# Moving the up projection's results to feature partitions through DRAM, and weaving the up and down projections job by job

## Chip, cores and metric

The kernel runs on one core of a Trainium2 chip. The metric is the device time of one execution in microseconds (us), lower is better. The engines are named as the profile names them: PE is TensorE's matmul side and PEld its weight load, DVE is VectorE, ACT is ScalarE, POOL is GpSimd, and SP (SPq) is SyncE, which here issues every DMA.

## What is computed

One layer of an encoder for 256 tokens of width 2048. Attention and RWKV mixing come first, then a projection back to the residual stream `x`; the change touches only the last part, the MLP:

```
h2 = rms_norm(x, norm_mlp[l])                                     # (256, 2048)
u  = square(relu(einsum('btd,df->btf', h2, mlp_up[l])))           # (256, 8192)
x  = x + einsum('btf,fd->btd', u, mlp_down[l])                    # (256, 2048)
```

All inputs are float32. Products are made with float32r operands: each factor is split into a rounded part (`hi`) and a rest (`lo`), and one product is three matmuls, hi by hi, hi by lo and lo by hi.

## The kernel before

The program first records all operations (class `Recorder`), then `plan` (L195) sorts them into one order with a cost model of its own: for each engine it takes the operation that can start first, ties by rank. Each engine, and SP for the DMAs, then works through its list strictly in that order.

**Jobs.** Every weight matrix is cut into jobs of 256 rows by 512 columns (512 KB). `load` (L502) issues a job's DMA into one of four `raw` buffers. `split` (L517) makes from `raw` the rounded part `hi` on ACT and the rest `lo` on DVE, each in one of three buffers, and then calls `load` for a later job, which needs the `raw` buffer just read. Splitting runs two jobs ahead of PE (`LOOK`).

**Plain jobs and jobs in seven products.** A plain job is two row blocks by two token halves by three matmuls: 12 matmuls of 512 columns. For up groups 3 to 15 (`QUICK`), the jobs whose number stands in `FAST` are done by a scheme of Strassen's kind over a 2 x 2 grid of blocks: seven block products in place of eight, each again three matmuls, so 21 matmuls of 256 columns (`seven`, L545). For that, `split` also builds four sums of weight blocks `T` with three DVE subtractions, and splits them into `Th` (ACT) and `Tl` (DVE). The matching sums of activation blocks `S` are built once, in `normal_h` (L1449). Job 0 of each group stays plain.

**Up groups.** `up_group(i)` (L1480) is eight jobs and gives 512 columns of `u`, 256 tokens by 512 features, in PSUM banks: two for groups 0 to 2, four from group 3 on, which `join` (L1483) combines to `C` in SBUF. The next projection needs features on partitions, so the result has to be transposed. `f` (L1500) applies the relu and at the same time moves 32 x 32 blocks to other partitions: 32 instructions on 32 partitions of 128 elements each, 26 of them on ACT (`EV`) and 6 on DVE, into `z`. Later `fin` (L1519) transposes `z` within 32 x 32 blocks on DVE to `uf`, squares it and splits it to a unit of `u`.

**Down groups.** A down group is four plain jobs on two units of `u` for 512 columns of the output, in two PSUM banks, added to `x2` by DVE. The tag of the banks, `acc` or `side` with four banks each, changes from group to group, so that one group's banks are read while the next group's are written.

**Order.** The loop at the end (L1545) runs group after group: one up group (8 jobs), two down groups (4 jobs each), and again; six down groups come last. `rank = -SPL` puts the splitting ahead of other work that could start at the same time.

The SBUF pool `f` has 18 slots of 4 KB per partition, which `x2`, `S`, `T`, `Th`, `Tl`, `C`, `q`, `z` and `uf` share.

## Time and profile before

| what | value |
|---|---|
| median of 3 runs | 1191.83 us (1191.58 to 1193.58) |
| the profiled execution, its own time | 1192.01 us |
| its span | 1190.2 us |
| PE busy | 1179.4 us (99%) |
| DVE busy | 974.1 us (82%) |
| ACT busy | 844.8 us (71%) |
| DMA queue q1, share of 16 engines' span | 60.0% |
| granted TensorE clock | full in all of 40 slices |

Read it so: the span is what the profiler saw from the first to the last instruction, and the execution's own time is 1.8 us longer. Busy time of PE is modelled and says that it had work, not that each matmul ran at its peak. Idle time of an engine off the critical path costs nothing. Instruction durations of DVE and ACT overlap with the next instruction's start by about 0.08 us, so a row's mean is a little more than what one instruction takes of the engine.

### The profile page before, as it was taken

What the parts mean: (1) busy time and instruction counts of PE and PEld (TensorE: products, weight loads), DVE (VectorE), ACT (ScalarE), POOL (GpSimd) and SP (SyncE); (2) the same over time, 40 slices, a digit from 0 to 9 for tenths busy, and PEclk for the clock granted to TensorE, in tenths of its full rate; (3) what the DMA queues carried; (4) which work ended last, traced back from release to release, by engine and by line L of the source; (5) the groups of instructions that cost most, each with busy time, mean ns of one, the idle gap of its engine ahead of it and who ended that gap; (6) DMA issues with size and microseconds to landing.
All of it is one profiled execution on the core that took longest, in us unless ns stands there. A gap on an engine that the chain in (4) does not pass through costs nothing.

```text
span 1190.2 us, 18141 instructions
## 1 busy us (share of the span) xinstructions
PE 1179.4 (99%) x6649; PEld 979.9 (82%) x6649; DVE 974.1 (82%) x1579; ACT 844.8 (71%) x1421; POOL 7.3 (1%) x31
## 2 busy tenths in 40 slices
PE   9999999999999999999999999999999999999998
PEld 6887887888778778788888888888888888888886
DVE  7789594896975976798988988988988998898864
ACT  7784566855687768999686777687677677677652
POOL 2000000000000000000000000000000000000000
PEclk9999999999999999999999999999999999999999
DMA  8655656256455445656666666666666666666663
GB/s 279 205 159 164 172 162 184 85 165 175 128 169 172 141 142 184 180 169 194 188 198 199 184 203 198 194 190 197 212 176 196 198 192 182 208 180 197 207 205 132
DMA packets 126297, 216.20 MB, mean 182 GB/s; under 512 B 21824, under 2 KB 24384, under 8 KB 126208
## 3 DMA queue, kind: packets, MB, share of 16 engines
q1 hardware_dynamic: 126208, 215.05, 60.0%
q8 instruction: 52, 0.85, 0.3%
q14 instruction: 37, 0.30, 0.1%
HBM read 211.09 MB, written 3.93 MB: 181 GB/s over the span
## 4 chain that ended last, share of the span: by engine, by line
PE 77%; DVE 10%; ACT 7%; DMA 3%; issue 3%; SPq 0%; DVEq 0%; ACTq 0%
PE acc L334 47%; PE side L334 23%; DVE lo L334 4%; PE sm L334 3%; PE tr L334 3%; ACT z L334 2%; ACT hi L334 2%; DVE Tl L334 2%; DVE T L334 2%; PE sm L179 2%; DMA raw<-up 1%; DMA raw<-w_in 1%; DVE x L334 1%; DVE uf L334 0%; DVE u L334 0%
## 5 line engine op out<-in xcount | busy, mean ns | idle before, releaser
L334 DVE TENSOR_TENSOR lo<-raw,hi 128x1024 fp32r<-128x1024 f32 (+3 forms) x460 | 462.7, 1015 | 151.3 <-ACT hi L334 148.7
L334 ACT CAST hi<-raw 128x1024 fp32r<-128x1024 f32 (+2 forms) x395 | 405.0, 1033 | 164.2 <-PE acc L334 106.8
L334 PE MATMUL acc<-hi,xT 128*128 128x512 f32 (+1 forms) x832 | 267.6, 396 | 0.6 <-ACT hi L334 0.6
L334 PEld LDWEIGHTS acc<-hi,xT 128*128 128x128 f32 x832 | 154.6, 190 | 33.8 <-ACT hi L334 1.7
L334 PE MATMUL acc<-lo,xT 128*128 128x512 f32 (+1 forms) x416 | 164.0, 394 | 0.7 <-DVE lo L334 0.6
L334 PE MATMUL acc<-hi,u 128*128 128x512 f32 x512 | 163.2, 395 | 0.0
L334 PE MATMUL side<-hi,u 128*128 128x512 f32 x512 | 163.1, 395 | 0.0
L334 ACT ACTIVATE z<-C 32x128 f32<-32x128 f32 x338 | 104.2, 308 | 39.4 <-DVE C L334 35.0
L334 ACT CAST Th<-T 128x1024 fp32r<-128x1024 f32 x65 | 68.2, 1050 | 71.0 <-DVE T L334 70.3
L334 PEld LDWEIGHTS acc<-hi,u 128*128 128x128 f32 x512 | 96.4, 188 | 22.4 <-DVE u L334 0.3
L334 PEld LDWEIGHTS side<-hi,u 128*128 128x128 f32 x512 | 96.5, 188 | 22.2
L334 PE MATMUL side<-lo,u 128*128 128x512 f32 x256 | 101.0, 395 | 0.0
L334 PE MATMUL acc<-lo,u 128*128 128x512 f32 x256 | 101.0, 394 | 0.0
L334 PEld LDWEIGHTS acc<-lo,xT 128*128 128x128 f32 x416 | 78.9, 190 | 18.2 <-DVE lo L334 2.2
L334 PE MATMUL side<-hi,hN 128*128 128x512 f32 (+1 forms) x328 | 91.7, 353 | 0.0
L334 PE MATMUL acc<-hi,hN 128*128 128x512 f32 (+1 forms) x308 | 83.4, 343 | 0.0
L334 DVE TENSOR_TENSOR Tl<-T,Th 128x1024 fp32r<-128x1024 f32 x65 | 79.1, 1216 | 0.0
L334 PEld LDWEIGHTS side<-hi,hN 128*128 128x128 f32 x328 | 59.7, 188 | 9.5
L334 PEld LDWEIGHTS acc<-hi,hN 128*128 128x128 f32 x308 | 55.5, 188 | 7.8
L334 PE MATMUL side<-lo,hN 128*128 128x512 f32 (+1 forms) x164 | 57.9, 353 | 0.0
L334 PEld LDWEIGHTS acc<-lo,u 128*128 128x128 f32 x256 | 48.2, 188 | 11.0
L334 PEld LDWEIGHTS side<-lo,u 128*128 128x128 f32 x256 | 48.2, 188 | 11.0
(310 smaller groups left out, 1874.0 us busy)
## 6 DMA issues: line engine op xcount, KB each, us to landing
raw<-up SPq DMA_DIRECT2D x128, 512.0 KB, 3.8
raw<-down SPq DMA_DIRECT2D x128, 512.0 KB, 4.4
raw<-w_in SPq DMA_DIRECT2D x93, 512.0 KB, 3.8
raw<-w_out SPq DMA_DIRECT2D x32, 512.0 KB, 3.9
raw<-w_in SPq DMA_DIRECT2D x8, 288.0 KB, 3.1
x<-x SPq DMA_DIRECT2D x4, 512.0 KB, 7.3
out<-x SPq DMA_DIRECT2D x8, 256.0 KB, 3.4
raw<-w_in SPq DMA_DIRECT2D x6, 256.0 KB, 5.8
```

Of the source, the lines that this page charges most:

```text
L179: p.fn(*p.args, **p.kw)
L334: op.fn(*op.args, **op.kw)
```

## The change

- `FAST` grows from five of the eight jobs to seven; only job 0 stays plain. Two more tiles `S` are built, and the first two lie in tiles of an earlier stage (`HOME`), not in pool `f`.
- `f` now applies the relu with one ACT instruction per token half (128 partitions by 512) into `zr`, writes `zr` to a DRAM tile `Zd` with two DMAs, and reads it back with four DMAs of 32 partitions each, in runs of 128 elements, into `z`. The 32 block instructions are gone, and `EV` with them. `fin` transposes and splits as before, but reads and writes in runs of 32 elements where the layout now differs.
- `gemm` becomes a generator `steps` that pauses after each job. From up group 3 on, the eight jobs of an up group and the eight of two down groups are woven by the string `WEAVE` (u for an up job, d for a down job): d d u d u d u u d u d u d u d u. Up groups have the `acc` banks and down groups the `side` banks, always.
- The last two additions of `join` become one instruction of 512 elements, and all of `join` gets the rank of the splitting.

```
--- before.py
+++ after.py
@@ -32,8 +32,7 @@
 NF = 18
 NRAW = 4
 LOOK = 2
-EV = 13
-FAST = (1, 2, 4, 5, 7)
+FAST = (1, 2, 3, 4, 5, 6, 7)
 QUICK = 3
 
 SPL = 120
@@ -476,7 +475,6 @@
                 advance(t)
 
     w_in, w_out, w_up, w_dn = A["w_in"], A["w_out"], A["up"], A["down"]
-    turn = [0]
 
     jobs = []
     cols = [(c + 512 * h, 512) for h in range(2) for c in (4096, 3072, 5120)] + [(c + 512 * h, 512) for h in range(2) for c in (0, 1024, 2048)]
@@ -491,12 +489,18 @@
     def fast(job):
         return job[0] is w_up and job[2] >= 512 * QUICK and job[1] // 256 in FAST
 
-    jobs += up_jobs(0) + up_jobs(1)
-    for e in range(8):
-        for j in range(4):
-            if e < 7 and not j % 2:
-                jobs += up_jobs(2 * e + 2 + j // 2)
-            jobs += [(w_dn, e * 1024 + 256 * k, 512 * j, 512) for k in range(4)]
+    def down_jobs(d):
+        return [(w_dn, d // 4 * 1024 + 256 * k, d % 4 * 512, 512) for k in range(4)]
+
+
+    WEAVE = "ddududuududududu"
+    for i in range(3):
+        jobs += up_jobs(i)
+    for i in range(3, 16):
+        ups, downs = up_jobs(i), down_jobs(2 * i - 6) + down_jobs(2 * i - 5)
+        jobs += [(ups if c == "u" else downs).pop(0) for c in WEAVE]
+    for d in range(26, 32):
+        jobs += down_jobs(d)
     raws, parts = deque(), deque()
 
     def load(between=None):
@@ -552,7 +556,7 @@
             return [u[:, i, k + kk, t * P:(t + 1) * P] for i in range(2)]
 
         def s(i):
-            return [S[:, j, i] for j in range(2)]
+            return [S[j][:, i] for j in range(2)]
 
         def b(kk, n):
             return [x[:, kk, n * 256:n * 256 + 256] for x in (hi, lo)]
@@ -568,10 +572,13 @@
             nc.tensor.matmul(o, x[0], y[1], start=False, stop=False, skip_group_check=True)
             nc.tensor.matmul(o, x[1], y[0], start=False, stop=end, skip_group_check=True)
 
-    def gemm(units, w, c0, ncols, evac, side=False, hooks={}, off=0):
-        turn[0] += w is w_up or w is w_dn
+    def gemm(*args, **kw):
+        for _ in steps(*args, **kw):
+            pass
+
+    def steps(units, w, c0, ncols, evac, side=False, hooks={}, off=0, tag="acc"):
         quick = [j for j in range(8) if fast((w, 256 * j, c0))]
-        acc = [bank("side" if turn[0] % 2 else "acc") for _ in range(4 if quick else 2)]
+        acc = [bank(tag) for _ in range(4 if quick else 2)]
         nu = 4 if w is not w_out and w is not w_dn else 2
         nh = 2 * nu
         for j in range(nh):
@@ -586,8 +593,7 @@
             if j in quick:
                 seven(acc, units[j // 2], 2 * j % 4, sums_[FAST.index(j)], (hi, lo, *T_), j == quick[0], j == quick[-1])
                 done(2)
-                continue
-            for kk in range(2):
+            for kk in range(0 if j in quick else 2):
                 k = 2 * j + kk
                 u = units[off + j // 2]
                 for t in range(2):
@@ -598,7 +604,10 @@
                     nc.tensor.matmul(o, xh, hi[:, kk, :ncols], start=(k == 0), stop=False, **more)
                     nc.tensor.matmul(o, xh, lo[:, kk, :ncols], start=False, stop=False, **more)
                     nc.tensor.matmul(o, xl, hi[:, kk, :ncols], start=False, stop=(k == 2 * nh - 1), **more)
+            if j < nh - 1:
+                yield
         evac(acc)
+        yield
 
     def rsqrt_small(out, ss, scale, bias):
 
@@ -1432,6 +1441,7 @@
         squares(x2[j], parts2, j)
 
     rows2 = []
+    HOME = {0: ("DW", "DA"), 1: ("X", "Sp")}
 
     def rstd_rows():
 
@@ -1457,14 +1467,19 @@
         for p in range(2):
             if 2 * j + p in FAST:
 
-                S, sr = ftile([P, 2, 4, P], "S", F32R), ftile([P, 4, P], "sr")
+                sr = ftile([P, 4, P], "sr")
+                if len(sums_) in HOME:
+                    S = [sm.tile([P, 512], F32R, tag=g, bufs=1, name=nm("S")).rearrange("p (s t) -> p s t", s=4) for g in HOME[len(sums_)]]
+                else:
+                    S = ftile([P, 2, 4, P], "S", F32R)
+                    S = [S[:, 0], S[:, 1]]
                 a1, a2 = a[:, 2 * p], a[:, 2 * p + 1]
                 nc.vector.tensor_add(sr[:, 0], a1[:, P:], a2[:, P:])
                 nc.vector.tensor_sub(sr[:, 1], sr[:, 0], a1[:, :P])
                 nc.vector.tensor_sub(sr[:, 2], a1[:, :P], a1[:, P:])
                 nc.vector.tensor_sub(sr[:, 3], a2[:, :P], sr[:, 1])
-                nc.scalar.copy(S[:, 0], sr)
-                nc.vector.tensor_sub(S[:, 1], sr, S[:, 0])
+                nc.scalar.copy(S[0], sr)
+                nc.vector.tensor_sub(S[1], sr, S[0])
                 sums_.append(S)
                 done()
         done()
@@ -1477,7 +1492,7 @@
     us = []
     pend = []
 
-    def up_group(i, hooks):
+    def up_group(i, hooks, tag="acc"):
 
 
         def join(acc):
@@ -1485,6 +1500,7 @@
             C, q = ftile([P, 2, 512], "C"), ftile([P, 3, 256], "q")
             lt, rt = slice(0, 256), slice(256, 512)
             b0, b1, b2, b3 = acc
+            nc.rank = -SPL
             nc.scalar.copy(q[:, 0], b2[:, lt])
             nc.vector.tensor_add(q[:, 2], q[:, 0], b2[:, rt])
             nc.vector.tensor_add(q[:, 1], q[:, 2], b3[:, lt])
@@ -1492,41 +1508,38 @@
             nc.vector.tensor_add(C[:, 0], qf[:, :512], b0)
             nc.vector.tensor_add(C[:, 1, lt], q[:, 2], b1[:, lt])
             nc.vector.tensor_add(C[:, 1, rt], q[:, 1], b1[:, rt])
-            nc.vector.tensor_add(C[:, 1, lt], C[:, 1, lt], b3[:, rt])
-            nc.vector.tensor_add(C[:, 1, rt], C[:, 1, rt], b3[:, rt])
+            c1 = C[:, 1].rearrange("p (n c) -> p n c", n=2)
+            nc.vector.tensor_add(c1, c1, b3[:, rt].unsqueeze(1).broadcast_to([P, 2, 256]))
+            nc.rank = 0
             done()
             return C
 
         def f(acc):
-            z = ftile([P, 4, 2, 4, 32], "z")
+            zr, z, Zd = ftile([P, 2, 512], "zr"), ftile([P, 8, P], "z"), dr.tile([T, 512], F32, name=nm("Zd"))
             C = join(acc) if i >= QUICK else None
             for t in range(2):
-                for tb in range(4):
-                    rows = slice(32 * tb, 32 * tb + 32)
-                    src = (C[:, t] if C is not None else acc[t]).rearrange("p (f c i) -> p f c i", c=4, i=32)
-                    for cb in range(4):
-                        o, s = z[32 * cb:32 * cb + 32, :, t, tb, :], src[rows, :, cb, :]
-                        r = rstd2[rows, t:t + 1]
-                        if 4 * tb + cb < EV:
-                            nc.scalar.activation(o, s, AF.Relu, **({} if i > 1 else dict(scale=r)))
-                        elif i > 1:
-                            nc.vector.tensor_scalar(o, s, 0.0, None, op0=ALU.max)
-                        else:
-                            nc.vector.tensor_scalar(o, s, r, 0.0, op0=ALU.mult, op1=ALU.max)
-            if C is not None:
-                done()
+                a = (C[:, t] if C is not None else acc[t]).rearrange("p (f c i) -> p c f i", c=4, i=32)
+                o = zr[:, t].rearrange("p (c f i) -> p c f i", c=4, i=32)
+                nc.scalar.activation(o, a, AF.Relu, **({} if i > 1 else dict(scale=rstd2[:, t:t + 1])))
+                nc.sync.dma_start(Zd[t * P:(t + 1) * P, :], zr[:, t])
+            Zv = Zd.rearrange("(g l) (c n) -> c l g n", l=32, c=4)
+            for c in range(4):
+                nc.sync.dma_start(z[32 * c:32 * c + 32], Zv[c])
+            done(1 if C is None else 2)
 
             def fin():
                 u = unit("u")
                 us.append(u)
-                uf = ftile([P, 4, T], "uf")
-                nc.vector.transpose(uf.rearrange("p f t -> p (f t)"), z.rearrange("p f t b i -> p (f t b i)"))
+                uf = ftile([P, 8, P], "uf")
+                nc.vector.transpose(uf.rearrange("p g n -> p (g n)"), z.rearrange("p g n -> p (g n)"))
                 nc.scalar.activation(uf, uf, AF.Square)
-                nc.scalar.copy(u[:, 0], uf)
-                nc.vector.tensor_sub(u[:, 1], uf, u[:, 0])
+                v = uf.rearrange("p g (f i) -> p f g i", i=32)
+                u0, u1 = (u[:, a].rearrange("p f (g i) -> p f g i", i=32) for a in range(2))
+                nc.scalar.copy(u0, v)
+                nc.vector.tensor_sub(u1, v, u0)
                 done(2)
             pend.append(fin)
-        gemm(hN if i > 1 else hT, w_up, 512 * i, 512, f, hooks=hooks)
+        return steps(hN if i > 1 else hT, w_up, 512 * i, 512, f, hooks=hooks, tag=tag)
 
     def store_evac(j):
         def f(acc):
@@ -1539,14 +1552,26 @@
         while pend:
             pend.pop(0)()
 
-    up_group(0, {2: lambda: make_h(3), 4: rstd_rows})
-    up_group(1, {2 * j: lambda j=j: normal_h(j) for j in range(4)})
+    def down_group(d):
+        e, j = d // 4, d % 4
+        return steps(us, w_dn, 512 * j, 512, store_evac(j) if e == 7 else add_evac(x2[j]), hooks={1: fin_hook}, off=2 * e, tag="side")
+
+    def run(*gens):
+        for g in gens:
+            yield from g
+
+    for _ in run(up_group(0, {2: lambda: make_h(3), 4: rstd_rows}),
+                 up_group(1, {2 * j: lambda j=j: normal_h(j) for j in range(4)}, "side")):
+        pass
     done()
-    for e in range(8):
-        for j in range(4):
-            if e < 7 and not j % 2:
-                up_group(2 * e + 2 + j // 2, {1: fin_hook})
-            gemm(us, w_dn, 512 * j, 512, store_evac(j) if e == 7 else add_evac(x2[j]), hooks={1: fin_hook}, off=2 * e)
+    for _ in up_group(2, {1: fin_hook}):
+        pass
+    for i in range(3, 16):
+        gens = {"u": up_group(i, {}), "d": run(down_group(2 * i - 6), down_group(2 * i - 5))}
+        for c in WEAVE:
+            next(gens[c])
+    for _ in run(*(down_group(d) for d in range(26, 32))):
+        pass
 
 
 def _constants(par):
```

The planner then places everything anew. Up to the first up group's results each engine's order is the same as before. Three places from the steady part follow; numbers behind the underscore tell tiles apart.

ACT before, where the results of an up group leave for `z` (`C` the joined sums, `hi` the split of weights):

```order
L334 COPY q_1422<-side_1382 128x256
L334 ACTIVATE z_1420<-C_1421 32x4x32
L334 CAST hi_1428<-raw_1407 128x1024
L334 ACTIVATE z_1420<-C_1421 32x4x32 x6
L334 CAST hi_1433<-raw_1413 128x1024
L334 ACTIVATE z_1420<-C_1421 32x4x32 x6
L334 CAST hi_1436<-raw_1416 128x1024
L334 ACTIVATE z_1420<-C_1421 32x4x32 x5
L334 CAST hi_1441<-raw_1419 128x1024
L334 ACTIVATE z_1420<-C_1421 32x4x32 x6
L334 CAST hi_1444<-raw_1427 128x1024
L334 ACTIVATE z_1420<-C_1421 32x4x32 x2
```

Here 26 block copies stand between five weight splits.

ACT now, at the same point (`q` a part of the join, `zr` the relu's result):

```order
L333 COPY q_1382<-acc_1311 128x256
L333 CAST hi_1388<-raw_1365 128x1024
L333 ACTIVATE zr_1378<-C_1381 128x512 x2
L333 CAST hi_1397<-raw_1371 128x1024
L333 CAST Th_1400<-T_1399 128x1024
L333 CAST hi_1403<-raw_1374 128x1024
```

In their place two instructions stand behind a single split.

SP before, from the last down jobs into an up group and to the next down group, all loads of weights:

```order
L334 DMA raw_1495<-down 128x2x512
L334 DMA raw_1503<-down 128x2x512
L334 DMA raw_1506<-up 128x2x512
L334 DMA raw_1511<-up 128x2x512
L334 DMA raw_1514<-up 128x2x512
L334 DMA raw_1519<-up 128x2x512
L334 DMA raw_1522<-up 128x2x512
L334 DMA raw_1525<-up 128x2x512
L334 DMA raw_1531<-up 128x2x512
L334 DMA raw_1541<-up 128x2x512
L334 DMA raw_1544<-down 128x2x512
```

The eight jobs of one up group follow each other here.

SP now, around the end of an up group (`Zd` in DRAM, `z` back in SBUF):

```order
L333 DMA raw_1377<-up 128x2x512
L333 DMA Zd_1380<-zr_1378 128x512
L333 DMA raw_1387<-up 128x2x512
L333 DMA Zd_1380<-zr_1378 128x512
L333 DMA raw_1390<-down 128x2x512
L333 DMA z_1379<-Zd_1380 32x8x128 x4
L333 DMA raw_1402<-up 128x2x512
L333 DMA raw_1405<-down 128x2x512
L333 DMA raw_1411<-up 128x2x512
L333 DMA raw_1417<-down 128x2x512
```

Two writes and four reads now stand between loads of weights, up and down jobs come in turns, and every load behind the reads is issued after them.

DVE now, from the end of `join` (first row) on:

```order
L333 TENSOR_TENSOR C_1381<-C_1381,acc_1312 128x512
L333 TENSOR_TENSOR lo_1389<-raw_1365,hi_1388 128x1024
L333 TENSOR_TENSOR T_1399<-raw_1371,T_1399 128x256
L333 TENSOR_TENSOR T_1408<-raw_1377 128x512
L333 TENSOR_TENSOR T_1408<-raw_1377,T_1408 128x256
L333 TENSOR_TENSOR lo_1398<-raw_1371,hi_1397 128x256
L333 TENSOR_TENSOR lo_1398<-raw_1371,hi_1397 128x512
L333 TENSOR_TENSOR Tl_1401<-T_1399,Th_1400 128x1024
L333 TENSOR_TENSOR T_1408<-raw_1377,T_1408 128x256
L333 TENSOR_TENSOR T_1414<-raw_1387 128x512
L333 TENSOR_TENSOR lo_1404<-raw_1374,hi_1403 128x1024
L333 TENSOR_TENSOR Tl_1410<-T_1408,Th_1409 128x1024
```

Two short instructions are left out here, and DVE goes on:

```order
L333 TENSOR_TENSOR lo_1407<-raw_1377,hi_1406 128x512
L333 TENSOR_TENSOR T_1414<-raw_1387,T_1414 128x256
L333 TENSOR_TENSOR lo_1413<-raw_1387,hi_1412 128x256
L333 TENSOR_TENSOR lo_1413<-raw_1387,hi_1412 128x512
L333 STREAM_TRANSPOSE uf_1392<-z_1379 128x1024
L333 TENSOR_TENSOR Tl_1416<-T_1414,Th_1415 128x1024
L333 TENSOR_TENSOR T_1423<-raw_1402 128x512
L333 TENSOR_TENSOR x_740_826<-x_740_826,side_1383 128x512
```

Three jobs' sums `T` (1399, 1408, 1414) are begun as soon as their weights are there, ahead of the rest of the splits in front of them, and the transpose of the `z` that came through DRAM stands 18 instructions behind the end of `join`, ahead of the next `Tl`.

## Rows read from the trace of the kernel before

**Rows 1.** The page's first part: busy time, share of the span, instructions.

```profile
PE 1179.4 (99%) x6649; PEld 979.9 (82%) x6649; DVE 974.1 (82%) x1579; ACT 844.8 (71%) x1421; POOL 7.3 (1%) x31
```

**Rows 2.** The chain in order of time: start us, us, what.

```profile
621.06 20.89 PE side L334 x141
641.95 11.15 PE acc L334 x48
653.10 11.15 PE side L334 x48
664.25 20.96 PE acc L334 x141
...
1175.06 10.46 PE acc L334 x45
```

**Rows 3.** Busy time by stage, two rounds of up, down, down.

```profile
621.06:664.25 43.19, 43.19 (x238) 37.36 (x238) 38.51 (x61) 31.43 (x51) 0.00 (x0) 1.00 0.65 195
664.25:707.53 43.28, 43.28 (x239) 37.38 (x238) 38.60 (x61) 31.53 (x51) 0.00 (x0) 1.00 0.63 194
```

**Rows 4.** DVE in order of time: start us, us, engine, line, operation.

```profile
669.22 1.22 DVE L334 TENSOR_TENSOR lo<-raw,hi 128x1024 fp32r<-128x1024 f32 x1
670.35 0.42 DVE L334 TENSOR_TENSOR T<-raw,T 128x256 f32<-128x256 f32 x1
670.69 0.42 DVE L334 TENSOR_TENSOR lo<-raw,hi 128x256 fp32r<-128x256 f32 x1
671.02 0.42 DVE L334 TENSOR_TENSOR T<-raw,T 128x256 f32<-128x256 f32 x1
671.36 0.69 DVE L334 TENSOR_TENSOR lo<-raw,hi 128x512 fp32r<-128x512 f32 x1
671.96 0.69 DVE L334 TENSOR_TENSOR T<-raw 128x512 f32<-128x512 f32 x1
672.56 0.42 DVE L334 TENSOR_TENSOR lo<-raw,hi 128x256 fp32r<-128x256 f32 x1
```

**Rows 5.** Groups of DVE and ACT instructions, 621.06 to 707.53 us (two rounds).

```profile
L334 DVE TENSOR_SCALAR z<-C 32x128 f32<-32x128 f32 x12 | 2.7, 222 | 0.3
...
L334 DVE STREAM_TRANSPOSE uf<-z 128x1024 f32<-128x1024 f32 x2 | 2.5, 1238 | 0.0
...
L334 ACT CAST hi<-raw 128x1024 fp32r<-128x1024 f32 x32 | 33.1, 1047 | 6.1 <-PE side L334 2.9 <-PE acc L334 2.9
L334 ACT ACTIVATE z<-C 32x128 f32<-32x128 f32 x52 | 16.0, 308 | 6.1 <-DVE C L334 5.4
```

**Rows 6.** Waits, the same two rounds: us in total, times, longest.

```profile
DVE lo L334 <- ACT hi L334: 7.6, 9, 1.8
...
DVE T L334 <- DMA raw<-up: 1.2, 2, 0.6
```

**Rows 7.** Tile raw, 600 to 1100 us.

```profile
L334 SPq DMA_DIRECT2D raw<-up x94: 367/368/368, 607.0 to 1098.9; - x94
...
  DMA raw<-up: 9.2, 13
...
DMA to landing us min/median/max: 3.5/4.1/6.0
```

**Rows 8.** Tile out (256 KB writes to DRAM).

```profile
DMA to landing us min/median/max: 2.2/3.4/5.2
```

**Rows 9.** Tile Nd (a small matrix through DRAM): writes, reads, landing.

```profile
L334 SPq DMA_DIRECT2D N<-Nd x4: 337/450/558, 135.6 to 286.2; - x4
...
DMA to landing us min/median/max: 2.2/3.7/5.2
```

**Rows 10.** DMA queues, 664 to 708 us.

```profile
DMA packets 4420, 8.56 MB, mean 194 GB/s; under 512 B 256, under 2 KB 256, under 8 KB 4418
...
q1 hardware_dynamic: 4418, 8.52, 62.8%
```

**Rows 11.** Busy time by stage, where the tiles S are built.

```profile
500.00:600.00 100.00, 99.43 (x477) 82.15 (x476) 90.35 (x148) 82.01 (x143) 0.00 (x0) 1.00 0.63 189
```

## The prediction
> **What bounds the kernel now.** I read the page's first part first [rows 1]: PE is busy for 99% of the span, DVE for 82%, ACT for 71%. The chain in order of time says what that means for the MLP [rows 2]: from 621 to 664 us it goes up group, down group, down group, each beginning where the last ended, and it goes on so to 1185.5 us (1175.06 + 10.46). Nothing but matmuls stands in it. Such a round of one up and two down groups takes 43.2 us, and there are 13 of them. The windows of two rounds [rows 3] say how far the other engines are from the bound: PE 43.23, DVE 38.56, ACT 31.48 us of a mean 43.23. DVE is 4.7 us short of PE, and the waits [rows 6] show that it spends them mostly waiting for ACT's `hi`, (7.6 + 1.2) / 2 = 4.4 us a round; PE does not wait for it. So a change helps here only if PE has less to do, and only as long as DVE can still keep up.
>
> **PE.** A down group is 48 matmuls of 512 columns in 11.15 us, 0.2323 us each [rows 2]. An up group is 36 such matmuls and 105 of 256 columns in 20.93 us (mean of the two): (20.93 - 8.36) / 105 = 0.1197 us each. A plain job is 12 x 0.2323 = 2.79 us, one in seven products 21 x 0.1197 = 2.51 us; the difference is 0.274 us. Two more jobs in each of 13 groups give 26 x 0.274 = **7.1 us**. A round falls to 42.68 us.
>
> **DVE.** From start to start an instruction of 1024 elements takes 1.14 us, of 512 elements 0.60, of 256 elements 0.34 [rows 4]. A plain split is one `lo`, 1.14. A split for seven products is T (0.60 + 2 x 0.34), `lo` (0.34 + 0.60) and `Tl` (1.14), together 3.36. Two more a round add 4.44. The six block copies on DVE go, 6 x 0.222 = 1.33 [rows 5], and the join's merged addition saves 2 x 0.34 - 0.60 = 0.08. So 38.56 + 4.44 - 1.33 - 0.08 = 41.6 us of 42.68. DVE stays under PE, but its room falls from 4.7 to 1.1 us a round.
>
> **ACT.** 26 of the 52 block copies of two rounds, 8.0 us a round, go [rows 5]. Two relu instructions of 512 elements come; the nearest rows are 0.308 us for 128 elements and 1.047 for 1024, which bound them, and a line between gives 0.63 each. Two more `Th` are 2 x 1.05 (the row of `hi`, the same size). 31.5 - 8.0 + 1.3 + 2.1 = 26.9 us: ACT gets more room, and this gives no time of itself, since PE does not wait for ACT.
>
> **The two more S.** Each is four operations of 128 elements, at most 0.34, and one of 512, 0.60: under 2 us each, 4 us once. Where they are built DVE is busy for 90% and PE for 99% [rows 11]; the block copies of up groups 0 to 2 that go there, 18 x 0.222 = 4.0 us, cover them. I put nothing down.
>
> **Banks.** Up groups now use the same four banks each time. The next up group's first job comes two down jobs, 5.6 us, after the last one. The join holds its banks `b0` and `b1` until the weight copy, two q, three C and one T that stand in front have run, some 0.4 + 2.9 = 3.3 us. Covered.
>
> **Where DVE is tightest.** An average is not enough when 1.1 us is left, so I follow DVE's list through a round. It is free of work when the second down group ends (job 15 of the weave), because its `x` additions need that. From there it has 41 instructions up to the `Tl` of job 10 of the next weave: 11 of 1024 elements, 13 of 512, 16 of 256 and the transpose of `z` (1.238 us less the overlap of 0.08 [rows 5]): 12.5 + 7.8 + 5.4 + 1.2 = 26.9 us. PE needs that `Tl` after job 16 (2.51), jobs 1 to 9 (24.27) and half of job 10's matmuls (1.2): 28.0 us, and some 0.4 goes for handing over from engine to engine at both ends. That leaves about 0.7 us. In between DVE waits for one load: T_1414 stands 3.7 us of DVE work (0.34 + 0.60 + 0.34 + 0.34 + 0.60 + 1.14 + 0.34) behind `lo_1389`, which frees the buffer of that load, and a load takes 0.37 us to issue and a median of 4.1 to land [rows 7]. Between 4.1 (if landing includes the issue) and 4.5 us against 3.7, DVE waits 0.4 to 0.8 us; before, it waited 9.2 / 13 = 0.7 us at such places [rows 7], and I take 0.8, the later end, since the queue gets busier. PE then loses 0.1 us a round, 1.3 us in all. The bounds are no loss (landing at the minimum of 3.5) and 2.2 us a round (landing at the maximum of 6.0 each time), which would be 28 us.
>
> **The way through DRAM.** On SP the six DMAs of a round stand among 16 loads of 0.37 us, so issuing is no limit. `z` must be there when DVE gets to the transpose. By the same walk relu 1 ends 0.8 us after the join; the second write is issued behind a load that needs `lo_1389`, 1.7 us after the join's end; 3.4 us to land [rows 8]; four reads of 0.45 us each on SP and 3.7 us from the last one's issue [rows 9]: 1.7 + 3.4 + 1.4 + 3.7 = 10.2 us. DVE has 17 instructions, 10.3 us, and the wait of 0.8 in front of the transpose. It is in time by 0.9 us, at medians. The loads behind the reads are not held up: their buffer is freed 7.4 us after the join (`lo_1404`, with the wait), the last read is issued after 1.7 + 3.4 + 1.8 = 6.9.
>
> **Sum.** The profiled execution took 1192.0 us, 0.2 over the median of the runs. 1192.0 - 7.1 + 1.3 = **1186.2 us**.
>
> **Rivals.** (a) *Loads land later.* 44 us carry 4418 packets in 62.8% of the 16 engines' time [rows 10], 0.10 us a packet. A round adds 256 packets of 2 KB and 1024 of 512 B: by bytes (1.05 of 8.5 MB) the share goes to 0.70, and if a small packet takes as long as a large one, to 0.81. With loads 0.3 to 0.7 us later, the wait at T_1414 goes straight to PE: 13 x 0.3 to 0.7 = 4 to 9 us, which gives 1190 to 1195, about no change. For it speaks that DVE has nothing left at job 10; against it that no matmul waited for a load in the rounds before.
> The Trainium skill (Perfetto Trace Analysis, DMA Optimizations) says that DMAs in pieces under 2 KB carry a heavy overhead per transfer; by that rule the reads in 512 B pieces put the share at the upper figure, 0.81, and the time at the upper end, 1195 us. The trace has few pieces so small in this stretch and cannot settle it, so it has part of this rival's chance.
> (b) *Slower: the transpose waits for `z`.* It stands in the middle of DVE's list, with every split behind it. If write and read land as late as the latest seen, 5.2 us each [rows 8, 9], `z` comes 1.8 + 1.5 = 3.3 us later, DVE waits 3.3 - 0.9 = 2.4 us, and PE loses it: 13 x 2.4 = 31 us, 1217 us. Halfway, 1.3 us late, it is 1203. It decides the sign from 0.9 us of margin + 0.45 us (7.1 - 1.3 over 13). Medians speak against it, the longer queue for it.
> (c) *The change does not do what it says.* The 2.51 us were read from up groups run alone; if a job in seven products among plain jobs takes as long as a plain one, nothing is saved on the two more, and the time is 1192.
>
> **Chances.** A measurement of this kernel can tell a change of about 0.2%, 2.4 us, from none. The forecast, with PE losing at most 0.3 us a round, 0.63, and its own range is 1184.5 to 1188.8. (a) 0.20, of which 0.07 still counts as faster, 0.08 as the same, 0.05 as slower. (b) 0.12, slower. (c) 0.05, the same. Faster 0.70, same 0.13, slower 0.17. The range goes from 1184.5, all of PE's saving and a little of the handing over, to 1196, the end of (a); left out are (b) and what lies beyond.
>
> **What would show it.** Right: down groups no longer have a chain piece of their own, rounds of 42.7 to 42.9 us in the chain, PE busy with no waits; DVE at 97% in those windows and its waits for `hi` down from 4.4 us to under 1; the relu under 0.7 us; loads still landing in about 4.1 us. Wrong: PE waiting for `Tl` or `lo` at job 8 or 10 of a round (a, by T_1414 waiting over 1.1 us), or the transpose waiting for a DMA of `z` (b), or matmuls of 256 columns over 0.12 us apart (c).

## Result and profile after

The changed kernel takes 1199.87 us, median of 6 runs (1196.68 to 1200.82), beside 1192.13 for the kernel before (6 runs, 1191.58 to 1193.58): ratio 1.0059 [1.0045, 1.0072]. It is slower by 0.6%, where 1186.2 with a range up to 1196 was forecast. The profiled execution took 1200.82 us, 8.8 more than that of before.

Page part 1 of the changed kernel, beside [rows 1]:

```profile
PE 1173.6 (98%) x6883; PEld 983.7 (82%) x6883; DVE 1012.2 (84%) x1610; ACT 765.7 (64%) x1065; POOL 7.3 (1%) x31
```

PE has 5.8 us less work (before 1179.4) and a span 8.8 us longer: it now waits. The length of a round is read from one row of the tile view of `q`, the first instruction of each of the 13 joins, of the first and the last. After:

```profile
L333 ACT COPY q<-acc x13: 364/373/375, 600.1 to 1127.8; 128x256 f32<-128x256 f32 x13
```

(1127.8 - 600.1) / 12 = 43.98 us a round. Before the same joins went from 598.4 to 1119.0, 43.38 a round. So the first join comes 1.7 us later and each round takes 0.6 more. The windows of three rounds from join to join, then of the stretch 600 to 1100, beside [rows 3] (columns: length, then busy us and count of PE, PEld, DVE, ACT, POOL; granted clock; DMA share; GB/s):

```profile
600.10:644.55 44.45, 42.89 (x254) 37.45 (x253) 41.59 (x63) 26.75 (x30) 0.00 (x0) 1.00 0.69 212
689.45:732.49 43.04, 42.75 (x257) 37.80 (x256) 41.64 (x64) 27.19 (x29) 0.00 (x0) 1.00 0.72 221
951.61:996.04 44.43, 43.09 (x257) 37.82 (x256) 41.82 (x64) 26.91 (x30) 0.00 (x0) 1.00 0.70 215
600.00:1100.00 500.00, 488.73 (x2888) 429.49 (x2887) 474.31 (x719) 306.65 (x320) 0.00 (x0) 1.00 0.70 216
```

DVE has the 41.6 us of work a round that were forecast, ACT 26.9. The clock is full throughout, so it plays no part. What is new stands in the waits of the same stretch, beside [rows 6] (us in total, times, longest):

```profile
PE acc L333 <- DVE Tl L333: 9.2, 11, 1.0
DVE T L333 <- DMA raw<-up: 8.9, 22, 0.7
DVE uf L333 <- DMA z<-Zd: 5.6, 6, 1.6
DVE uf L333 <- DMA raw<-up: 4.5, 4, 1.4
...
DVE Tl L333 <- ACT Th L333: 2.0, 11, 0.2
```

The 500 us hold 500 / 43.98 = 11.4 rounds. DVE waits 8.9 us at `T` and 5.6 + 4.5 + 0.6 (one more row, put down to issue) = 10.7 us at the transpose `uf`, 1.7 a round together. With 41.6 to 41.8 of work that is 43.3 to 43.5 of 43.98, and PE waits for DVE's `Tl` 11 times. One round shows both, on DVE:

```profile
953.77 0.69 DVE L333 TENSOR_TENSOR T<-raw 128x512 f32<-128x512 f32 x1 [0.47 <-DMA raw<-up]
...
956.30 0.68 DVE L333 TENSOR_TENSOR C<-C,acc 128x512 f32<-128x512 f32 x1
...
962.46 0.69 DVE L333 TENSOR_TENSOR T<-raw 128x512 f32<-128x512 f32 x1 [0.35 <-DMA raw<-up]
...
969.19 1.25 DVE L333 STREAM_TRANSPOSE uf<-z 128x1024 f32<-128x1024 f32 x1 [1.21 <-DMA raw<-up]
```

and on SP, which issues the DMAs:

```profile
958.57 0.46 SPq L333 DMA_DIRECT2D Zd<-zr  x1
960.71 0.37 SPq L333 DMA_DIRECT2D raw<-down  x1
963.15 1.81 SPq L333 DMA_DIRECT2D z<-Zd  x4
965.00 0.45 SPq L333 DMA_DIRECT2D raw<-up  x1
```

The join ends at 956.98 and the second write is issued 1.6 us later, as forecast. The reads can be issued only when it has landed, 4.6 us later at 963.15, and at 969.19, 6.0 us after that, the transpose starts. DVE was there at 967.98, 11.0 us after the join, as forecast. The wait is put down to a load that lands at about the same time, but the transpose reads only `z`. The trace has a landing for each read: the last one here, issued at 964.5, landed 4.4 us later at 968.9, and in all 13 rounds the transpose starts 0.0 to 0.3 us after the last read of `z` landed. So I count these waits as `z`'s, whichever name they have. The median landings are the last columns of page part 6 (KB each, us from issue to landing), beside [rows 7 to 9]:

```profile
raw<-up SPq DMA_DIRECT2D x128, 512.0 KB, 4.4
...
Zd<-zr SPq DMA_DIRECT2D x32, 256.0 KB, 4.4
z<-Zd SPq DMA_DIRECT2D x64, 128.0 KB, 3.8
```

In the stretch 600 to 1100 all loads together went from a median of 4.1 to 4.4; over the whole span those of `up` went from 3.8 to 4.4, those of `down` from 4.4 to 4.5. The write and the read of the way through DRAM are new. The forecast had priced them by other transfers, 3.4 and 3.7; they take 4.4 and 3.8, and the last of the four reads, which decides, a median of 4.2.

### The profile page after: what moved, and what is told of

It is laid out like the page before. It is cut to its first block, busy times and chain, and to the rows that moved or that the text cites. A ratio compares the mean times of both kernels' runs of the same rounds, so it can differ in the third digit from the quotient of the medians.

```text
span 1199.0 us, 18503 instructions
## 1 busy us (share of the span) xinstructions
PE 1173.6 (98%) x6883; PEld 983.7 (82%) x6883; DVE 1012.2 (84%) x1610; ACT 765.7 (64%) x1065; POOL 7.3 (1%) x31
## 2 busy tenths in 40 slices
DMA packets 148314, 233.01 MB, mean 194 GB/s; under 512 B 23360, under 2 KB 42304, under 8 KB 148224
## 3 DMA queue, kind: packets, MB, share of 16 engines
q1 hardware_dynamic: 148224, 231.83, 64.0%
## 4 chain that ended last, share of the span: by engine, by line
PE 52%; DVE 25%; DMA 10%; ACT 6%; issue 5%; SPq 1%; DVEq 0%; ACTq 0%
PE acc L333 32%; PE side L333 14%; DVE lo L333 10%; DMA raw<-up 5%; DVE T L333 4%; DVE Tl L333 3%; PE tr L333 2%; PE sm L333 2%; DMA z<-Zd 2%; ACT hi L333 2%; DMA Zd<-zr 2%; PE sm L178 2%; DVE C L333 1%; DVE u L333 1%; DMA raw<-w_in 1%
## 5 line engine op out<-in xcount | busy, mean ns | idle before, releaser
L333 PE MATMUL side<-hi,u 128*128 128x512 f32 x1024 | 335.9, 394 | 0.0
L333 PEld LDWEIGHTS side<-hi,u 128*128 128x128 f32 x1024 | 192.7, 188 | 41.4
L333 PE MATMUL side<-lo,u 128*128 128x512 f32 x512 | 202.8, 396 | 2.9 <-DVE lo L333 2.9
L333 PE MATMUL acc<-hi,hN 128*128 128x256 f32 (+1 forms) x532 | 134.6, 317 | 0.0
L333 PE MATMUL acc<-Th,S 128*128 128x256 f32 x546 | 112.3, 281 | 0.0
L333 PEld LDWEIGHTS acc<-Th,S 128*128 128x128 f32 x546 | 90.1, 188 | 0.0
L333 PE MATMUL acc<-Tl,S 128*128 128x256 f32 x273 | 78.2, 286 | 11.3 <-DVE Tl L333 11.2
L333 PE MATMUL acc<-lo,hN 128*128 128x256 f32 (+1 forms) x266 | 84.6, 318 | 0.9 <-DVE lo L333 0.9
L333 DVE TENSOR_TENSOR T<-raw,T 128x256 f32<-128x256 f32 x182 | 76.6, 421 | 2.3
L333 DVE TENSOR_TENSOR T<-raw 128x512 f32<-128x512 f32 x91 | 62.5, 687 | 15.4 <-DMA raw<-up 15.0
```

The source lines that it names most:

```text
L333: op.fn(*op.args, **op.kw)
```

## Experiments

My theory after the result: PE's saving is real, but DVE has some 1 us of room a round, and each wait of its fixed list for a DMA beyond that goes to PE; the waits are for `z` first, for loads second. Rivals: the traffic itself is what costs; DVE simply has too much work; the weave is at fault, not the trip; the order that the planner makes from too early landing times is. The planner lays out every list anew for each edit, so a difference between two kernels holds the edit and the new order; this turned out to matter. Only both_late_plan came out inside the range of its theory, and nine of the sixteen runs came out in no range that was stated before them.

| run | edit | median us | ratio to before |
|---|---|---|---|
| no_trip | no DMAs, the transpose reads `zr` | 1180.87 | 0.9901 [0.9886, 0.9916] |
| trip_unread | DMAs made, the transpose reads `zr` | 1186.66 | 0.9949 [0.9934, 0.9963] |
| six_fast | job 4 plain again | 1214.00 | 1.0175 [1.0160, 1.0191] |
| five_fast | jobs 3 and 6 plain again | 1215.04 | 1.0178 [1.0148, 1.0208] |
| pool_queue | the six DMAs issued by POOL | 1214.95 | 1.0187 [1.0171, 1.0203] |
| nraw5 | a fifth `raw` buffer | 1210.60 | 1.0158 [1.0132, 1.0185] |
| block_copies | block copies back, all on ACT | 1215.27 | 1.0192 [1.0175, 1.0209] |
| pool_sub | `u`'s rest on POOL | 1238.71 | 1.0387 [1.0371, 1.0402] |
| z_late_plan | plan: trip's DMAs 1.0 us later | 1196.98 | 1.0041 [1.0028, 1.0054] |
| fin_later | `fin` in every second down group only | 1209.29 | 1.0138 [1.0117, 1.0159] |
| fin_later_loads | that, and plan: loads 0.8 later | 1196.23 | 1.0034 [1.0022, 1.0046] |
| both_late_plan | plan: trip 1.0, loads 0.8 later | 1186.16 | 0.9952 [0.9935, 0.9970] |
| both_later_plan | plan: trip 1.5, loads 1.2 later | 1206.01 | 1.0119 [1.0098, 1.0139] |
| before_late_plan | kernel before, plan: loads 0.8 later | 1196.42 | 1.0038 [1.0025, 1.0051] |
| five_late_plan | five_fast and both_late_plan | 1202.20 | 1.0091 [1.0073, 1.0109] |
| block_late_plan | block_copies, plan: loads 0.8 later | 1213.05 | 1.0176 [1.0163, 1.0189] |

### Is it the trip, and which part of it?

no_trip:

```
-                nc.sync.dma_start(Zd[t * P:(t + 1) * P, :], zr[:, t])
-            Zv = Zd.rearrange("(g l) (c n) -> c l g n", l=32, c=4)
-            for c in range(4):
-                nc.sync.dma_start(z[32 * c:32 * c + 32], Zv[c])
...
-                nc.vector.transpose(uf.rearrange("p g n -> p (g n)"), z.rearrange("p g n -> p (g n)"))
+                nc.vector.transpose(uf.rearrange("p g n -> p (g n)"), zr.rearrange("p a n -> p (a n)"))
```

> Leaves out the way through DRAM: the transpose reads the relu's result zr where it lies, so the 32 x 32 blocks stay in the wrong partitions; the output is not the reference's. DVE, ACT and PE have the same instructions as in the changed kernel; the six DMAs a round are gone. Theory (waits): 1183 to 1187 us, rounds of 42.7 to 42.9. Rival (work): 1196 to 1200. Rival (traffic): loads land in 4.1 us again (4.4 with the trip), and the time falls to 1183 to 1190 too.

trip_unread has the last two lines alone. (In both, the calls of `done`, which count free slots of pool `f` while the program is recorded, move accordingly.)

> The writes to Zd and the reads of z are made as in the changed kernel, but nobody uses z: the transpose reads zr where it lies (blocks stay in wrong partitions, the output is not the reference's). Of the 19 us that the way through DRAM costs (1199.9 against 1180.9 without it), this keeps the traffic and the place on SP's list and takes away the transpose's wait. Theory z (the wait for z at the transpose is the cost): 1181 to 1184 us. Theory loads (the reads and writes hold up SP or the DMA engines, and loads of weights come late): 1190 to 1199, with DVE's waits for loads still 0.7 us a round or more.

no_trip is 19.0 us faster than the changed kernel and 11.3 faster than before. Its windows (the stretch, and a round):

```profile
600.00:1100.00 500.00, 499.14 (x2990) 442.47 (x2989) 488.27 (x744) 315.33 (x330) 0.00 (x0) 1.00 0.65 197
852.74:895.29 42.55, 42.55 (x257) 37.71 (x256) 41.47 (x64) 26.78 (x30) 0.00 (x0) 1.00 0.65 200
```

and its joins, (1108.1 - 597.3) / 12 = 42.57 us a round:

```profile
L333 ACT COPY q<-acc x13: 361/373/375, 597.3 to 1108.1; 128x256 f32<-128x256 f32 x13
```

So the weave and the two more jobs in seven products do what was said of them: PE is full at 42.6 us a round, with DVE at 41.5. The rivals "the weave" and "DVE has too much work" fall for seven jobs in seven products. trip_unread, with all the traffic and no reader, gives 13.2 of the 19.0 us back; 5.8 stay. By these two runs the larger part goes with the transpose's dependence on `z`, the rest with the traffic and its places on SP. They do not separate these two from each other, nor from the new order of each run.

### Does more room on DVE help?

```
-FAST = (1, 2, 3, 4, 5, 6, 7)
+FAST = (1, 2, 3, 5, 6, 7)
```

> Six of eight jobs in seven products (1, 2, 3, 5, 6, 7), weave and the way through DRAM as changed. PE 42.95 us a round, DVE 41.7 - 2.2 = 39.5. Theory (waits): 39.5 + 2.0 of waits is under 42.95, so PE bounds again: 1192 - 3.6 = 1188.4, and up to 2 us more for the first rounds, 1188 to 1191. Rival (work): the same, 1188 to 1191. Rival (traffic): the DMAs are the same as in the changed kernel, and the time stays above 1194.

five_fast:

```
-FAST = (1, 2, 3, 4, 5, 6, 7)
+FAST = (1, 2, 4, 5, 7)
...
-    HOME = {0: ("DW", "DA"), 1: ("X", "Sp")}
+    HOME = {}
```

> Five of eight jobs in seven products as before, weave and the way through DRAM as changed. PE 43.23 us a round as before, DVE 41.7 - 4.4 = 37.3. Theory (waits) and rival (work): PE bounds with room to spare, 1190 to 1193 us. Rival (traffic): late loads hold PE up still, over 1195.

Both are 14 to 15 us slower than the changed kernel, with less work on DVE and more waits. Of six_fast, the waits of the whole span:

```profile
DVE T L333 <- DMA raw<-up: 54.3, 51, 2.6
...
DVE uf L333 <- DMA z<-Zd: 18.1, 14, 3.1
```

Over the whole span the changed kernel had 15.0 us in 24 waits in the first of these places and 10.3 in 8 in the second. I read this so, and no run tests it: the new order puts each `T` so early that its load has not come, and since the load behind it is issued only when DVE has freed a buffer, late stays late. Room on average is not room where the wait stands. By its number (above 1194 and 1195) the rival "traffic" came true in both; both_late_plan below, with the same DMAs, speaks against it as the cause. In five_fast the granted clock has a mean of 0.994, which is 7.3 us of its 1217.4 at most, by estimate.

### Other places for the trip

```
-                nc.sync.dma_start(Zd[t * P:(t + 1) * P, :], zr[:, t])
+                nc.gpsimd.dma_start(Zd[t * P:(t + 1) * P, :], zr[:, t])
...
-                nc.sync.dma_start(z[32 * c:32 * c + 32], Zv[c])
+                nc.gpsimd.dma_start(z[32 * c:32 * c + 32], Zv[c])
```

> The six DMAs of the way through DRAM are issued by POOL, which is idle, so that no load of weights stands behind them on SP. Theory z: the transpose still waits, 1194 to 1202. Theory loads by SP's list: loads are free, 1183 to 1190. Theory loads by traffic: no change, 1195 to 1202.

nraw5 (pool `f` gives up a slot):

```
-NF = 18
-NRAW = 4
+NF = 17
+NRAW = 5
```

> Five raw buffers in place of four (and 17 slots in pool f in place of 18, for the room), else the changed kernel: each load is issued about one job earlier. Theory z: the waits for loads (0.75 us a round) go, the wait for z stays, 1190 to 1198. Theory loads: 1183 to 1190.

block_copies has the `f` and `fin` of the kernel before, each block instruction on ACT:

```
-                        if 4 * tb + cb < EV:
+                        if True:
                             nc.scalar.activation(o, s, AF.Relu, **({} if i > 1 else dict(scale=r)))
```

> Undoes the way through DRAM alone: 32 block copies a group as before the change, all on ACT, with seven jobs in seven products and the weave as changed. DVE has the same work as in the changed kernel, ACT 26.9 - 1.3 + 32 x 0.308 = 35.5 us of a round. Theory (any wait for DMA on DVE's list goes to PE): no DMA stands in the chain any more, 1181 to 1186 us. Rival (ACT): ten us of copies between the splits on ACT's list make hi and Th late, and DVE, which has one us of room, waits for them: 1190 or more.

pool_sub:

```
-                nc.vector.tensor_sub(u1, v, u0)
+                nc.gpsimd.tensor_sub(u1, v, u0)
```

> The changed kernel with one instruction of DVE (the rest of u, 1024 elements, once a round) given to POOL, which is idle: DVE 40.5 of 42.6 us. Theory (DVE has no room for its 2.3 us of waits): with 1.1 us more room PE loses 1.1 us a round less, 1185 to 1190 us. Rival (waits grow into any room, as with six_fast): 1196 to 1202.

All four lose, and not in the rounds alone: the first join comes at 605.9 us in nraw5, 606.1 in pool_queue, 604.2 in block_copies and 603.2 in pool_sub, after 600.1 in the changed kernel. pool_queue takes the trip from SP's list, and `T` then waits 42.8 us in 48 for loads over the whole span; nraw5 waits 22.2 in 22 there and 10.2 for `z`. In nraw5 the granted clock matters too: its mean is 0.992, with 0.83 from 200 to 230 us, where the changed kernel has the full clock; PE had stood idle for 1.3 us of the 7 before it fell (205 to 212). Of 1207.5 us of span that is 9.7 us at most, by estimate, so most of the 10.7 us by which nraw5 is slower than the changed kernel can be the clock's, and the run says little of the fifth buffer. In block_copies nothing waits for a trip, but ACT does 14 copies in a row ahead of the splits that PE needs (its timeline, then PE's wait):

```profile
800.17 4.46 ACT L333 ACTIVATE z<-C 32x128 f32<-32x128 f32 x14
```

```profile
PE side L333 <- ACT hi L333: 13.0, 12, 1.2
```

Over the span PE waits 13.0 us so. That is near the 15.4 us by which the run is slower than the changed kernel, but it is not a share of them: the changed kernel has waits of its own, 11.2 us at `Tl`, which are gone here, and 4.1 us lie before the first join. That ACT's list is the cause is argued from these waits, not shown; no run takes the copies apart. pool_sub is under the unexpected things at the end.

### Is it the order?

z_late_plan changes only what the planner supposes of the trip's DMAs:

```
-            done = dma + 0.9
+            kind = op.outs[0].tensor.name.split("_")[0]
+            done = dma + 0.9 + {"z": 1.0, "Zd": 1.0, "raw": 0.0}.get(kind, 0.0)
```

> The planner is told that the writes to Zd and the reads of z land 1.0 us later than it supposed; the work is the same, only the order changes, and the transpose moves back on DVE's list. Theory (waits): in the changed kernel DVE is busy 41.7 us of a round of 44.0, and its list waits 1.26 us a round for z and 0.75 us for loads, with every split behind it; without the wait for z a round falls to 42.8 to 43.0 us, 1184 to 1189 us. Rival (work): DVE's work as such, with two jobs of lead, is too much whatever it waits for; 1197 to 1201. Rival (traffic): the extra megabyte a round makes the loads late; loads still land in 4.4 us and the time stays at 1197 to 1201.

The wait of `uf` is gone from the stretch 600 to 1100, but others stand in its place: `T` for loads 8.2 us in 24, `lo` for `hi` 6.4, `u` for ACT 5.3. It is 2.9 us faster than the changed kernel, not some 13: PE still waits 9.3 us in 11 for `Tl`. Taking away the wait for `z` is not enough.

fin_later lets `fin` stand only in the second down group of a round:

```
-        return steps(us, w_dn, 512 * j, 512, store_evac(j) if e == 7 else add_evac(x2[j]), hooks={1: fin_hook}, off=2 * e, tag="side")
+        return steps(us, w_dn, 512 * j, 512, store_evac(j) if e == 7 else add_evac(x2[j]), hooks={1: fin_hook} if d % 2 or d > 25 else {}, off=2 * e, tag="side")
```

> The transpose of z and what follows it is called for in the second down group of a round in place of the first, some 20 us after the join in place of 10; the work and the DMAs are the same. Theory z (the wait for z in the middle of DVE's list): no wait is left there, 1184 to 1190 us. Rival (another wait takes its place, as with z_late_plan, because the six DMAs still hold up SP and the loads): 1194 to 1199, with more waiting for loads.

fin_later_loads adds to it

```
-            done = dma + 0.9
+            done = dma + 0.9 + {"z": 0.0, "Zd": 0.0, "raw": 0.8}.get(kind, 0.0)
```

> As fin_later, and the planner is told that loads of weights land 0.8 us later than it supposed (its 3.5 us become 4.3, near the measured 4.4), so that T is not put on DVE's list before its load is there. Theory (waits on DVE's list, whichever they are): 1183 to 1187 us. Rival (DVE's 41.6 us of 42.6 is too full by itself once the DMAs of the way through DRAM run beside it): 1192 or more.

fin_later loses: `T` waits 16.3 us in 36 (600 to 1100), and `uf` still 11.9. It is 9.4 us slower than the changed kernel. With the later loads in the plan it gets 13.1 us faster, 3.6 under the changed kernel.

The planner supposes a landing after a start of 1.1 us, the bytes at 360,000 per us and 0.9 us more (L299, L300): 3.5 us for a load, 2.7 for a write, 2.4 for a read, on an idle queue. Measured were 4.4, 4.4 and 3.8.

both_late_plan differs from the changed kernel in this line alone (`kind` as above):

```
-            done = dma + 0.9
+            done = dma + 0.9 + {"z": 1.0, "Zd": 1.0, "raw": 0.8}.get(kind, 0.0)
```

> The planner is told of both, 1.0 us more for the way through DRAM and 0.8 us more for loads; the place where the transpose is called for is as in the changed kernel. Theory (waits): 1184 to 1189 us. Rival (another wait takes its place): 1194 to 1199.

The same work and the same traffic as the changed kernel, in another order, take 1186.16 us (1184.31 to 1189.21), faster than both kernels. Its stretch, waits in it, joins (42.75 us a round), and one transpose, whose join ended at 860.64:

```profile
600.00:1100.00 500.00, 498.57 (x2980) 441.33 (x2979) 486.01 (x739) 317.03 (x328) 0.00 (x0) 1.00 0.72 222
```

```profile
DVE T L334 <- DMA raw<-up: 5.1, 11, 0.8
DVE lo L334 <- ACT hi L334: 4.2, 10, 0.9
...
PE acc L334 <- DVE Tl L334: 1.2, 2, 0.8
DVE uf L334 <- DMA z<-Zd: 0.9, 2, 0.7
```

```profile
L334 ACT COPY q<-acc x13: 372/373/374, 598.8 to 1111.8; 128x256 f32<-128x256 f32 x13
```

```profile
875.96 1.25 DVE L334 STREAM_TRANSPOSE uf<-z 128x1024 f32<-128x1024 f32 x1
```

The transpose starts 15.3 us after the join's end, where the changed kernel's was due after 11.0, and no longer waits. Landing medians are the same as after (loads 4.4, writes 4.4, reads 3.7), the DMA share even higher. So neither the traffic nor late landing costs those 13.7 us by itself; the order does. It is not DVE's list alone that differs: here the second write is issued 3.9 us after the join's end and the reads 8.7 after it (changed kernel 1.6 and 6.2), so `z` lands later than there, and DVE comes later still. z_late_plan has much the same places, no wait for `z` in this stretch, and 1197.0 us; it lacks only the later loads. Which of the moved places is worth how much, no run shows.

Four runs ask how far this carries. both_later_plan:

```
+            done = dma + 0.9 + {"z": 1.5, "Zd": 1.5, "raw": 1.2}.get(kind, 0.0)
```

> The changed kernel, the planner told 1.2 us more for loads (4.7) and 1.5 more for the way through DRAM. Theory: what waits are left in both_late_plan (0.55 us a round on DVE for loads and z) go, 1182 to 1186 us. Rival (supposing later only moves work back): 1186 to 1192.

before_late_plan has the line of fin_later_loads (`raw` 0.8) in the kernel before:

> The kernel before the change, its planner told that loads land 0.8 us later. There PE bounds with 4.7 us of room on DVE, and waits for loads cost PE nothing. Theory (a wait costs only where DVE has no room): 1190.5 to 1193, no change. Rival (the planner's landing times cost every kernel of this form): 1184 to 1188, and the change gives nothing of its own.

five_late_plan has the line of both_late_plan in five_fast:

> five_fast (1215 us: PE 43.23 us a round, DVE 37.3) with the planner told 0.8 us more for loads and 1.0 more for the way through DRAM. Theory (the order made from optimistic landing times): PE bounds, 1189 to 1194 us. Rival (the weave or the way through DRAM is slow by itself when fewer jobs are in seven products): 1205 or more.

block_late_plan has the line of fin_later_loads in block_copies:

> block_copies (1215 us) with the planner told 0.8 us more for loads. Theory (order from optimistic landing times): 1183 to 1188 us, as no_trip or little over it. Rival (ACT: ten us of block copies between the splits make hi and Th late): 1200 or more, with PE waiting for hi.

Supposing still later landings loses 19.9 us again: `uf` waits 23.2 us in 10 in 600 to 1100. SP issues the reads later there, but above all they take longer. The new order has a load right in front of them, one round on SP and then the page's median:

```profile
881.44 0.37 SPq L334 DMA_DIRECT2D raw<-down  x1
881.91 1.89 SPq L334 DMA_DIRECT2D z<-Zd  x4
```

```profile
z<-Zd SPq DMA_DIRECT2D x64, 128.0 KB, 6.6
```

The reads land after 6.6 us, where the changed kernel's and both_late_plan's took 3.8 and 3.7; there the last load was issued 2.1 to 2.9 us before the reads (in all 13 rounds of the first and 12 of the second), here 0.5 to 0.8 in all 13. This order has lengthened the very landings that the planner was told of. The kernel before gets 4.4 us slower. Five jobs in seven products get 12.8 us faster, but stay 10 us over before; over their span `T` still waits 35.3 us in 17 for loads, up to 4.2, and `uf` 13.2 in 9 for reads that stand right behind a load again and take 6.6 us. The block copies gain 2.2 us, the wait for ACT's `hi` is still there. So later landing times are no rule that makes orders good; they made one good order here.

## Why the prediction was wrong

**Right.** PE's work: 42.68 us a round forecast, 42.57 with nothing to wait for (no_trip), so (c) fell. DVE's work 41.6 (41.59 to 41.82), ACT's 26.9 (26.75 to 27.19); the room of 1.1 us was there. The second write's issue (1.6 us after the join, forecast 1.7) and the moment DVE gets to the transpose (11.0 against 11.1) came as walked.

**Failed: "It is in time by 0.9 us, at medians."** In the round shown the write took 4.6 us, not 3.4, and from the first read's issue to the transpose 6.0 passed, not 1.4 + 3.7 = 5.1. With the write issued 0.1 earlier than walked, `z` came 2.0 us later than priced, and 0.9 of margin became 1.2 of waiting. The prices came from other places than the rounds. [rows 8] are eight writes of the result at the end of the kernel before, where the DMA share is low (the writes, then the window of that stretch):

```profile
L334 SPq DMA_DIRECT2D out<-x x8: 332/357/357, 1152.9 to 1187.0; - x8
...
1150.00:1190.00 40.00, 36.21 (x156) 29.01 (x154) 18.44 (x19) 11.54 (x11) 0.00 (x0) 1.00 0.48 161
```

[rows 9] are 16 writes of 64 KB and 4 reads of 128 KB together, between 113 and 286 us, where the share is 0.57 (135 to 290). In the rounds after the change it is 0.69 to 0.72. The same eight writes still take 3.6 us in the changed kernel, so what lies between 3.4 and 4.4 is mostly the place that the row came from. And 3.7 is the median of reads on their own, where the last of four landed after 4.2. Whether the share alone makes the difference, no run shows. Over the span the transpose waited 10.3 us in 8 for `z`, 6.1 in 5 put down to loads and 0.6 to issue: 17.0 us in 14 times. That is rival (b), to which the prediction gave 0.12, near its "halfway" size of 1203.

**Failed: "PE then loses 0.1 us a round."** The 0.4 us that this walk put down for handing over came from no row; in the trace of before, PE starts 0.06 us after the DVE instruction that it waited for, and DVE 0.04 us after PE's (medians). PE lost 43.98 - 42.68 = 1.3 us a round, 13 x 1.3 = 17 us, against the 15.9 by which saving and result differ (7.1 + 8.8). The wait at `T` was about the 0.8 forecast (8.9 / 11.4 = 0.8 a round), though now in two places. With the wait at `uf` that makes 1.7 us of waits a round against 1.1 of room: 0.6 of the 1.3 that PE lost. Since the rest is not traced to a single wait, that all of it comes from the wait for `z` is argued, not shown.

**(a), loads later:** they did land 0.3 us later, but both_late_plan has the same landings without the loss. By bytes a share of 0.70 was forecast, by packets 0.81: it is 0.69 to 0.72. Over the whole span the transfers of q1 took 7.5% more time (64.0% of 1199.0 us against 60.0% of 1190.2) for 7.8% more bytes (231.83 MB against 215.05) and 17% more packets (148224 against 126208). The price that I gave the 512 B pieces by the Trainium skill (Perfetto Trace Analysis, DMA Optimizations) is not borne out here; they took share by their bytes.

**What I did not see** is that one order is one draw. The chances took the lists as given and priced lateness by medians; the same work takes 1186.2 us in one order, 1199.9 and 1206.0 in others. That both_late_plan came out at the forecast time bears out the sum of the work, not the forecast for the order that it was made for.

**Open.** Which properties make an order good: one bad one is seen, reads right behind a load, but the changed kernel does not have it, and none of the runs gives a rule. Why five jobs under the weave stay slow with the corrected plan. How the 5.8 us of trip_unread divide between traffic and SP. And since each run has its own order, 13.2 and 5.8 are differences of two orders too.

## What to carry to other kernels

When an engine is left with 3% of room, the sum of its work no longer gives the time: walk its fixed list, and give every instruction that needs a DMA a landing time for the queue as the change will load it, not as it was. A planner's supposed landing times are part of such a kernel: measure the landings again after each change of the traffic, look at what the queue has been given just before a transfer that someone waits for, plan again, and time several orders before a change is judged. Take the price of a transfer from rows in the same stretch, or say that it comes from another.

## Unexpected on the chip

While POOL does a float32 subtraction, a DVE subtraction beside it is held until it is over. In pool_sub:

```profile
810.69 2.61 POOL L333 TENSOR_TENSOR u<-uf,u 128x1024 fp32r<-128x1024 f32 x1 [44.13 <-ACT u L333]
810.94 2.64 DVE L333 TENSOR_TENSOR T<-raw,T 128x256 f32<-128x256 f32 x1
```

The DVE instruction takes 0.42 us alone, 2.64 here; it ends 0.28 us after POOL's. It is so in all 13 rounds, 2.63 to 2.65 us each. The 182 of this kind take DVE 105.2 us, where the changed kernel's take 76.6: 28.6 more, for 16 x 1.22 = 19.5 freed by the move. How much of the 38.8 us by which this run is slower comes from that, how much from its new order, and how much from the clock, was not taken apart: the granted clock has a mean of 0.989 here, which is 13.6 us of its 1237.3 at most, by estimate.

Reads of 128 KB that are issued right behind a load of 512 KB took about 3 us longer to land. In both_later_plan, five_late_plan, z_late_plan and both_late_plan, 148 reads of `z` stand in groups of four whose first was issued less than 1 us after the issue of a load. From issue to landing their medians, run by run, are 6.4 to 6.9 us; those of the other 108 are 3.4 to 4.1. That the load in front is the cause is read from this split; no run moves it alone.
